# w_down of an expert in one double slot, the first gate weights by rows, and another order of the last products, squares and stores in a hybrid attention and mixture-of-experts block

## The chip, the cores and the metric

The kernel runs on one core of a Trainium2 chip. A core has five engines, each with its own instruction queue: TensorE (PE: matmuls, with the weight loads shown apart as PEld), VectorE (DVE), ScalarE (ACT), GpSimd (POOL) and SyncE (SP, which here does nothing but issue DMAs). Sixteen DMA engines move data between HBM and SBUF (the on-chip memory of 128 partitions); matmuls write into PSUM banks. The engines meet only through semaphores. The metric is the device time of one execution in microseconds.

## The reference

The input is `x` of 256 tokens by 1024 features, in fp32. Cut to what matters:

```python
h = rmsnorm(x, g1)
z = h @ w_in                      # q, k, v, gates, HGRN2 inputs, merge gates
a = nsa_mixer(z...)               # compressed, selected and windowed attention
b = hgrn2_mixer(z...)             # a gated linear recurrence
x = x + merge(a, b) @ w_out
h = rmsnorm(x, g2)
# 4 groups of 8 experts; group softmax, 2 experts of each token's group
for e in range(32):
    y = (silu(h @ w_gate[e]) * (h @ w_up[e])) @ w_down[e]   # 1024x512, 1024x512, 512x1024
    x = x + weight[:, e] * y      # zero where the token is not routed to e
out = rmsnorm(x, g_final)
```

Each expert has 2 MB of `w_gate`, 2 MB of `w_up` and 2 MB of `w_down`: 192 MB for the 32 experts, and all of it is read.

## The kernel before, in words

**Front (0 to 240 us).** The projection weights come as 1 MB stripes `raw<-in_wf` of 128x2048. Each stripe is split into two parts: ACT writes the high part (`whi`, L275), DVE the low part (`wlo`, L279), and PE multiplies with three matmuls for each pair (L416, L418, L419). `split()` keeps two stripes ahead, and `split_part` holds the ACT half of a split back until a matmul of an earlier stripe (`marks[-HOLD]`). The last stripes are `n0`, `n1` (merge gates) and `o00`, `o10`, `o01`, `o11` (`pwo`, the output projection). Norm, routing and the gather of tokens follow (`pga`, L1113).

**Experts (240 us to the end).** Eight groups `q` of four experts. A group takes `hidden(q)`: the gate product into `pg` and the up product into `pu` (both L1225 in `product`), silu and the product of both in `h`; then `prepare(q + 1)`, the routing of the next group; then `down(q)`: `py` (L1279), the weighting and the split of the result into `ys` (L1261 on ACT, L1262 on DVE), and the scatter into four PSUM banks `acc[tt][n]` (L1267; tt a tile of 128 tokens, n a half of the columns). The last group has `down_last` instead (L1293): first columns 0:512, then 512:768 and 768:1024. `finish` makes the last rmsnorm: `square` (ACT, L1334), `scaled` (DVE, L1339: acc times the row of the norm's gains), sum and power on POOL (L1345, L1346), the scaling by DVE and ACT (L1347, L1349) and four stores of 256 KB, two on SP's queue and two on ACT's.

**Weights and slots.** All expert weights go through SP's queue, which works its DMAs off in order: an issue that waits holds up all that stand behind it. `load_expert(n)` (L310, L320, L324) issues the next n pieces of a list: per group eight gate pieces, eight up pieces, eight w_down pieces, of 1 MB each (8 KB in each of 128 partitions). They lie in the pool `big` of `WSLOTS` = 25 slots of 1 MB, which the stripes and their split parts share. `product` frees four slots and asks for four pieces after each half (16 matmuls in the program, 32 in the trace, which shows two records for each), `down` likewise. How many pieces are issued during the front, and behind which stripe, is set by the table `EARLY` and by one call of `load_expert(25 - sum(EARLY.values()))`. The last group's w_down is loaded by columns: 0:512 of all four row blocks (1 MB each, runs of 2 KB), then two times 256 columns (512 KB each, runs of 1 KB).

**Order.** Each engine's instruction order is laid down at build time by a scheduler that follows the program order and estimated times. Within `overflow()` (L1404), a branch that is not taken in this run, the slot `y` is used too, so the first write of the output tile `y` (L1339) waits until SP's queue has passed that branch.

Of the kernel before, what the change touches and what calls it, by code (L numbers as in the profile page):

```python
# [163 lines left out]
WSLOTS = 25  # L164
# [7 lines left out]
CUTS = [slice(0, 256), slice(256, 512)]  # L172
GATE_V = (0, 0)
EARLY = {"m20": 1, "h1": 3, "o00": 1, "m21": 1, "m00": 2, "o11": 2, "m01": 2, "m31": 2, "h0": 1, "o01": 2}
# [5 lines left out]
def tile_block(ctx, tc, x, xp, xa, xb, wf, wcmp, vec, rows, consts, lmask, w_gate, w_up, w_down, out, dbg=None, manual=False):  # L180
# [11 lines left out]
    def slot(name, dtype=F32):  # L192
        return big.tile([128, 2048], dtype, tag="w", name=name)

# [99 lines left out]

    pieces = []
    for q in range(NE // 4):
        for i in range(6):
            pieces += [(4 * q + e, i) for e in range(4)]

    def load_expert(n=1):  # L300

        for _ in range(n):
            if pieces:
                e, i = pieces.pop(0)
                hf = i % 2
                t = slot("we")
                if i < 4:
                    store, src = ((WG, w_gate), (WU, w_up))[i // 2]
                    store[e, hf] = t.rearrange("p (k c) -> p k c", k=4)
                    nc.sync.dma_start(store[e, hf], src[e].rearrange("(p k) c -> p k c", k=8)[:, 4 * hf:4 * hf + 4])  # L310
                elif e >= NE - 4:

                    w = t.rearrange("p (k c) -> p k c", k=4)
                    WD[e, hf] = w
                    for c in CUTS if hf else [WHOLE]:
                        tails.append((w, e, hf, c))
                else:
                    w = t.rearrange("p (k c) -> p k c", k=2)
                    WD[e, hf] = w
                    nc.sync.dma_start(w, w_down[e].rearrange("(p k) c -> p k c", k=4)[:, 2 * hf:2 * hf + 2])  # L320
                if len(tails) == 12:
                    tails.sort(key=lambda x: (x[2], x[3].start, x[1]))
                    for w, e, hf, c in tails:
                        nc.sync.dma_start(w[:, :, c], w_down[e, :, 512 * hf:512 * hf + 512].rearrange(  # L324
                            "(p k) c -> p k c", k=4)[:, :, c])
                    tails.clear()

    tails = []
# [14 lines left out]
    hh_, hl_ = slot("hh_", F32R), slot("hl_", F32R)  # L343
# [8 lines left out]
    rr = cp.tile([128, 2], F32, name="rr")  # L352
    cbr = cp.tile([128, 2, 8, 5], F32, name="cbr")
# [866 lines left out]
    def product(q, W, p):  # L1220

        for hf in range(2):
            for k in range(4):
                for e in range(4):
                    i = PE.matmul(p[32 * e:32 * e + 32], xes[q][:, 4 * hf + k, 32 * e:32 * e + 32], W[4 * q + e, hf][:, k],  # L1225
                                  start=hf == 0 and k == 0, stop=hf == 1 and k == 3, skip_group_check=True)
            load_expert(4)
# [45 lines left out]
    def down(q):  # L1273
        py = [bank(t, "py") for t in ("ns", "pj")]
        for kh in range(2):
            for j in range(2):
                for n in range(2):
                    for e in range(4):
                        PE.matmul(py[n][32 * e:32 * e + 32], hTs[q][:, 2 * kh + j, 32 * e:32 * e + 32],  # L1279
                                  WD[4 * q + e, kh][:, j, 512 * n:512 * n + 512], start=kh == 0 and j == 0,  # L1280
                                  stop=kh == 1 and j == 1, skip_group_check=True)
            load_expert(4)
# [5 lines left out]
    def down_last(q):  # L1288

        def columns(n, c, p):  # L1290
            for j in range(4):
# [136 lines left out]
```

## Time and profile before

| | |
|---|---|
| median of three runs | 687.94 us (687.25 to 688.8) |
| the profiled execution | 686.17 us, of which the span from first to last instruction is 684.2 us |
| mean granted TensorE clock | 0.946 of full speed |
| busy: PE, PEld, DVE, ACT, POOL | 84%, 46%, 31%, 21%, 5% of the span |
| moved by DMA | 238.85 MB, mean 349 GB/s |

Engine shares are means over the whole span, and the stages differ: up to 240 us the projections and attention run, behind it the experts. What lies between the span and the run's own time (2 us) is start and end outside the instructions. In the rows further down, "idle before <- X" tells what ended an engine's idle time before an instruction.

### The profile page before, as it was taken

The numbers are of one execution on the slowest core, as the hardware profiler recorded it, in microseconds if no ns is written. First come the engines' busy times: TensorE is split into PE (matmuls) and PEld (weight loads), VectorE is DVE, ScalarE is ACT, GpSimd is POOL, SyncE is SP. The second block draws the span as 40 slices with busy tenths as digits, with TensorE's granted clock in tenths as the row PEclk, the third lists the DMA queues.
The fourth block names the chain that finished last, engine by engine and source line by source line (L and its number), as shares of the span: only waits on it lengthen the run. The fifth ranks groups of instructions, "written<-read, shape, count | busy, mean of one in ns | idle before, by whom it ended". The sixth has DMA issues, their size and how long they took to land. (4 is left out here: it accounts for less than half of the span.)

```text
span 684.2 us, 8830 instructions
## 1 busy us (share of the span) xinstructions
PE 576.8 (84%) x3692; PEld 317.8 (46%) x3692; DVE 212.1 (31%) x430; ACT 145.2 (21%) x231; POOL 32.5 (5%) x47
## 2 busy tenths in 40 slices
PE   8999999999999999987779668787766877796674
PEld 7988778888997834342132114223211421231111
DVE  5886656668567431121011002201100210110012
ACT  6433558474364210100000000000000000000002
POOL 0323202000000100000000000000000000000001
PEclk9999999999999999999899989989998998898898
DMA  8963534846748989999999999999999999999993
GB/s 340 406 249 123 185 124 152 341 182 230 287 165 309 421 332 420 419 420 420 420 420 420 417 421 420 420 420 420 420 418 419 420 421 420 421 419 421 406 366 114
DMA packets 39788, 238.85 MB, mean 349 GB/s; under 512 B 4032, under 2 KB 8640, under 8 KB 12608
## 3 DMA queue, kind: packets, MB, share of 16 engines
q1 hardware_dynamic: 39312, 237.19, 85.9%
q10 hardware_dynamic: 432, 1.05, 0.4%
q8 instruction: 31, 0.51, 0.3%
q14 instruction: 13, 0.11, 0.0%
HBM read 237.17 MB, written 1.05 MB: 348 GB/s over the span
## 5 line engine op out<-in xcount | busy, mean ns | idle before, releaser
L1225 PE MATMUL pu<-we,xe 128*32 128x512 f32 x512 | 98.3, 715 | 35.0 <-DMA we<-in_w_up 31.8
L1225 PE MATMUL pg<-we,xe 128*32 128x512 f32 x512 | 95.4, 689 | 35.2 <-DMA we<-in_w_gate 35.2
L1279 PE MATMUL py<-we,hT 128*32 128x512 f32 x448 | 76.2, 596 | 9.4 <-DMA we<-in_w_down 9.3
L1249 DVE SCALAR_TENSOR_TENSOR h<-pu,wv,h 128x512 f32<-128x512 f32 x8 | 8.7, 1089 | 227.3 <-PE pu L1225 227.3
L279 DVE TENSOR_TENSOR wlo<-raw,whi 128x2048 fp32r<-128x2048 f32 (+3 forms) x34 | 67.6, 1995 | 23.3 <-ACT whi L275 23.2
L1225 PEld LDWEIGHTS pu<-we,xe 128*32 128x32 f32 x512 | 21.3, 127 | 107.2 <-DMA we<-in_w_up 60.2
L1225 PEld LDWEIGHTS pg<-we,xe 128*32 128x32 f32 x512 | 20.5, 123 | 105.0 <-DMA we<-in_w_gate 65.3
L1261 ACT ACTIVATE ys<-py,wv 128x512 fp32r<-128x512 f32 (+1 forms) x17 | 11.2, 662 | 264.4 <-PE py L1279 232.4
L275 ACT ACTIVATE whi<-raw 128x2048 fp32r<-128x2048 f32 (+3 forms) x34 | 56.1, 1663 | 37.4 <-PE pxs L419 12.5
L419 PE MATMUL pws<-hh__93,wlo 128*128 128x256 f32 x192 | 48.4, 284 | 0.5 <-DVE wlo L279 0.5
L418 PE MATMUL pws<-hl__94,whi 128*128 128x256 f32 x192 | 48.5, 284 | 0.0
L1279 PEld LDWEIGHTS py<-we,hT 128*32 128x32 f32 x448 | 19.8, 109 | 59.6 <-issue 35.5
L1262 DVE SCALAR_TENSOR_TENSOR ys<-py,wv,ys 128x512 fp32r<-128x512 f32 (+1 forms) x17 | 12.2, 719 | 93.0 <-ACT ys L1261 92.3
L1243 ACT ACTIVATE h<-pg,wv 128x512 f32<-128x512 f32 x8 | 9.2, 1148 | 134.9 <-PE pg L1225 134.8
L419 PEld LDWEIGHTS pws<-hh__93,wlo 128*128 128x128 f32 x192 | 36.7, 191 | 0.7 <-DVE wlo L279 0.7
L418 PEld LDWEIGHTS pws<-hl__94,whi 128*128 128x128 f32 x192 | 36.7, 191 | 0.2 <-issue 0.2
L416 PE MATMUL pws<-hh__93,whi 128*128 128x256 f32 x192 | 33.3, 293 | 0.9 <-ACT hh__93 L375 0.9
L1113 PE MATMUL pga<-lm,x 128*128 128x128 f32 x256 | 30.3, 276 | 0.0
L418 PE MATMUL pxs<-wlo,hh__93 128*128 128x512 f32 (+1 forms) x80 | 29.8, 375 | 0.0
L419 PE MATMUL pxs<-whi,hl__94 128*128 128x512 f32 (+1 forms) x80 | 29.5, 372 | 0.0
L1113 PEld LDWEIGHTS pga<-lm,x 128*128 128x128 f32 x256 | 29.3, 192 | 0.2 <-DVE lm L1104 0.2
L416 PEld LDWEIGHTS pws<-hh__93,whi 128*128 128x128 f32 x192 | 26.6, 191 | 4.7 <-issue 1.9
(246 smaller groups left out, 655.4 us busy)
## 6 DMA issues: line engine op xcount, KB each, us to landing
we<-in_w_gate SPq DMA_DIRECT2D x64, 1024.0 KB, 19.9
we<-in_w_up SPq DMA_DIRECT2D x64, 1024.0 KB, 19.9
we<-in_w_down SPq DMA_DIRECT2D x60, 1024.0 KB, 19.9
raw<-in_wf SPq DMA_DIRECT2D x27, 1024.0 KB, 5.2
we<-in_w_down SPq DMA_DIRECT2D x8, 512.0 KB, 9.4
raw<-in_wf SPq DMA_DIRECT2D x2, 560.0 KB, 11.8
raw<-in_wf SPq DMA_DIRECT2D x2, 512.0 KB, 5.7
x<-in_x SPq DMA_DIRECT2D x2, 512.0 KB, 9.4
```

What stands on the lines that cost most here:

```text
L275: i = S.activation(his[n][:, c], raws[n][:, c], AF.Copy)
L279: splits.append((i, V.tensor_tensor(los[n][:, c], raws[n][:, c], his[n][:, c].bitcast(F32), op=OP.subtract)))
L416: PE.matmul(out_, lh, rh, start=start and i == 0, stop=False, skip_group_check=True)
L418: PE.matmul(out_, lh, rl, start=False, stop=False, skip_group_check=True)
L419: last = PE.matmul(out_, ll, rh, start=False, stop=stop and i == n - 1, skip_group_check=True)
L1113: i = PE.matmul(pgs[q, n][:, 128 * k:128 * k + 128], xv[:, tt, 512 * n + 128 * k:512 * n + 128 * k + 128], sel[q][:, tt], start=tt == 0 an ...
L1225: i = PE.matmul(p[32 * e:32 * e + 32], xes[q][:, 4 * hf + k, 32 * e:32 * e + 32], W[4 * q + e, hf][:, k], start=hf == 0 and k == 0, stop=h ...
L1243: S.activation(h, pg.rearrange("p (c j) -> p c j", j=4), AF.Silu, scale=r)
L1249: V.scalar_tensor_tensor(h, pu.rearrange("p (c j) -> p c j", j=4), r, h, op0=OP.mult, op1=OP.mult)
L1261: return (S.activation(hi[:, c], p[:, c], AF.Copy, scale=wv), V.scalar_tensor_tensor(lo[:, c], p[:, c], wv, hi[:, c].bitcast(F32), op0=OP. ...
L1262: V.scalar_tensor_tensor(lo[:, c], p[:, c], wv, hi[:, c].bitcast(F32), op0=OP.mult, op1=OP.subtract))
L1279: PE.matmul(py[n][32 * e:32 * e + 32], hTs[q][:, 2 * kh + j, 32 * e:32 * e + 32], WD[4 * q + e, kh][:, j, 512 * n:512 * n + 512], start=kh ...
```

## The change

- **Slots.** The pool has 17 slots of 1 MB and four "pairs" of 2 MB, the same sum. A split stripe's two parts lie in one pair, and so do the two parts of the normed input (`hhl`). The whole w_down of an expert lies in one pair and comes by one DMA of 2 MB (16 KB in each partition). `down(q)` runs its products over all four row blocks, gives the four pairs back at its end and then asks for four pieces.
- **First group.** Its gate weights come as eight pieces by row block `k`: each has that row block of all four experts (2 KB runs). The gate product of group 0 frees one slot and asks for one piece after each four matmuls. The order of the first group is eight gate pieces, three up, one w_down, four up, three w_down, one up, and `EARLY` is set anew.
- **Last w_down.** Per expert row blocks 0 and 1 with all columns (1 MB, 8 KB runs), then row blocks 2 and 3 in columns 0:512 (512 KB, 2 KB runs), 512:768 and 768:1024 (256 KB each, 1 KB runs).
- **End.** `down_last` multiplies row blocks 0 and 1 of all three column spans first, then 2 and 3 span by span. Squares and `scaled` of columns 0:768 are made in parts as the spans come; `finish` squares the last 256 columns (tile 0 on ACT, tile 1 on DVE), and scales in parts on DVE and ACT. One store of 512 KB per token tile, both on SP's queue.

```diff
-WSLOTS = 25
+WSLOTS = 17
+PAIRS = 4
+LAST = [(slice(0, 2), slice(0, 1024)), (slice(2, 4), slice(0, 512)), (slice(2, 4), slice(512, 768)), (slice(2, 4), slice(768, 1024))]
...
+    def pair(name, dtype=F32):
+
+        return big.tile([128, 4096], dtype, tag="w2", bufs=PAIRS, name=name)
...
-            his[n] = slot("whi", F32R)[:, :WIDTH[n]]
-            los[n] = slot("wlo", F32R)[:, :WIDTH[n]]
+            his[n], los[n] = [t[:, :WIDTH[n]] for t in two(pair("wsp", F32R), 2048)]
...
+                if kind == "k":
+                    WG[i] = slot("we").rearrange("p (e c) -> p e c", e=4)
+                    nc.sync.dma_start(WG[i], w_gate[0:4].rearrange("e (p k) c -> p e k c", k=8)[:, :, i])
...
+                    WD[e] = pair("wd").rearrange("p (k c) -> p k c", k=4)
+                    if e < NE - 4:
+                        nc.sync.dma_start(WD[e], w_down[e].rearrange("(p k) c -> p k c", k=4))
+                    elif e == NE - 1:
+                        load_last()
...
+                if 4 * hf + k in W and q == 0:
+                    load_expert(1)
+            if 4 * hf not in W or q:
+                load_expert(4)
...
+        for i in range(3):
+            products(i, (0, 1))
+        for i, (n, c) in enumerate(spans):
+            products(i, (2, 3))
+            if i < 2:
+                ys = parts_of()
+            weighted(q, n, c, py[i], ys)
+            scatter(q, n, c, ys)
+            if i < 2:
+                for tt in range(2):
+                    square(tt, n, c)
+                    scaled(tt, n, c)
...
+        c = CUTS[1]
+        ss, f = [st[:, 8 + tt:9 + tt] for tt in range(2)], [st[:, 10 + tt:11 + tt] for tt in range(2)]
+        S.activation(scr[0][:, c], acc[0][1][:, c], AF.Square, scale=1 / 32, accum_out=ss[0])
+        V.tensor_copy(scr[1][:, c], acc[1][1][:, c])
+        V.scalar_tensor_tensor(scr[1][:, :256], acc[1][1][:, c], 1 / 1024, scr[1][:, c], op0=OP.mult, op1=OP.mult,
+                               accum_out=ss[1])
...
+            nc.sync.dma_start(out[128 * tt:128 * tt + 128, :], y)
...
-    load_expert(25 - sum(EARLY.values()))
+    load_expert(20 - sum(EARLY.values()))
```

SP's queue at the end of the front stands so before (`raw` a stripe, `x_2058` the input tile, `we` a slot with expert weights):

```order
L261 DMA raw<-in_wf 128x2048 x4
L223 DMA x_2058<-in_xp 128x1024 x2
L310 DMA we<-in_w_up 128x2048 x4
L320 DMA we<-in_w_down 128x2048 x8
L310 DMA we<-in_w_gate 128x2048 x8
L310 DMA we<-in_w_up 128x2048 x8
```

and so in the changed kernel (`wd` a pair with the w_down of one expert):

```order
L267 DMA raw<-in_wf 128x2048 x3
L324 DMA wd<-in_w_down 128x4096
L267 DMA raw<-in_wf 128x2048
L229 DMA x_2030<-in_xp 128x1024 x2
L320 DMA we<-in_w_up 128x2048 x4
L324 DMA wd<-in_w_down 128x4096 x3
L320 DMA we<-in_w_up 128x2048
L320 DMA we<-in_w_gate 128x2048 x8
```

The first w_down piece now stands ahead of the last stripe, and the last piece of group 0 ahead of the first gate piece of group 1 is an up piece of 1 MB. On VectorE, early in the front (about 14 to 24 us of the trace before; `prx` is a PSUM tile with the first norm's row factors, `rxb` its copy, `hg` a projection of HGRN2), this is the order before:

```order
L384 SCALAR_TENSOR_TENSOR xa,st<-x 128x1024
L497 TENSOR_TENSOR lbt<-vc__70 128x4
L391 TENSOR_SCALAR rxt<-cs,st 128x128 x2
L500 TENSOR_SCALAR lbt<-lbt 128x4
L279 TENSOR_TENSOR wlo<-raw,whi 128x2048
L400 COPY rxb<-prx 128x256
L516 TENSOR_TENSOR hg_301<-pws,rxb 128x512
```

and this in the changed kernel:

```order
L503 TENSOR_TENSOR lbt<-vc__70 128x4
L390 SCALAR_TENSOR_TENSOR xa,st<-x 128x1024
L506 TENSOR_SCALAR lbt<-lbt 128x4
L397 TENSOR_SCALAR rxt<-cs,st 128x128 x2
L406 COPY rxb<-prx 128x256
L285 TENSOR_TENSOR wsp<-raw,wsp 128x2048 x2
L522 TENSOR_TENSOR hg_299<-pws,rxb 128x512 x2
```

The copy of `prx` now stands ahead of the low part of that stripe (`wsp<-raw,wsp`) instead of behind it. On TensorE, the last instructions before are:

```order
L1293 MATMUL py<-we,hT 32x512 x16
L1293 MATMUL py<-we,hT 32x256 x5
L1267 MATMUL acc<-ys,sT 128x512 x2
L1293 MATMUL py<-we,hT 32x256 x4
L1267 MATMUL acc<-ys,sT 128x512 x2
L1293 MATMUL py<-we,hT 32x256 x16
L1267 MATMUL acc<-ys,sT 128x256 x2
L1293 MATMUL py<-we,hT 32x256 x4
L1267 MATMUL acc<-ys,sT 128x256 x2
L1293 MATMUL py<-we,hT 32x256 x3
L1267 MATMUL acc<-ys,sT 128x256 x4
```

and in the changed kernel:

```order
L1306 MATMUL py<-wd,hT 32x512 x8
L1306 MATMUL py<-wd,hT 32x256 x16
L1306 MATMUL py<-wd,hT 32x512 x8
L1306 MATMUL py<-wd,hT 32x256 x5
L1277 MATMUL acc<-ys,sT 128x512 x2
L1306 MATMUL py<-wd,hT 32x256 x4
L1277 MATMUL acc<-ys,sT 128x512 x2
L1277 MATMUL acc<-ys,sT 128x256 x4
L1306 MATMUL py<-wd,hT 32x256 x7
L1277 MATMUL acc<-ys,sT 128x256 x4
```

Half of each span's products stand ahead of the others; of the last span seven products and its four scatter matmuls stand behind the scatter of the span before it.

## Rows read from the trace of the kernel before

**Rows 1.** The page's second part: the span in 40 equal slices of 17.1 us, busy tenths of PE and of the DMA engines, and GB/s.

```profile
PE   8999999999999999987779668787766877796674
DMA  8963534846748989999999999999999999999993
GB/s 340 406 249 123 185 124 152 341 182 230 287 165 309 421 332 420 419 420 420 420 420 420 417 421 420 420 420 420 420 418 419 420 421 420 421 419 421 406 366 114
```

**Rows 2.** The page's sixth part: DMA issues, count, size of each, median us from issue to landing.

```profile
we<-in_w_gate SPq DMA_DIRECT2D x64, 1024.0 KB, 19.9
we<-in_w_down SPq DMA_DIRECT2D x60, 1024.0 KB, 19.9
```

**Rows 3.** Waits of SP's queue: us in total, times, longest.

```profile
SPq L310 <- DMA we<-in_w_gate: 113.9, 54, 3.3
SPq L310 <- PE pg L1225: 14.0, 7, 11.9
```

**Rows 4.** Timeline of SP's queue, 205 to 260 us: start, length of the merged group, issues.

```profile
217.50 14.95 SPq L320 DMA_DIRECT2D we<-in_w_down  x8
244.25 5.24 SPq L310 DMA_DIRECT2D we<-in_w_gate  x8
```

**Rows 5.** Stretches from the front's end into the experts: window, its length, busy us of PE, PEld, DVE, ACT and POOL, granted clock, DMA share, GB/s.

```profile
232.00:240.00 8.00, 7.54 (x84) 6.89 (x84) 5.58 (x28) 1.26 (x4) 0.81 (x2) 1.00 1.01 421
240.00:242.00 2.00, 2.00 (x23) 0.98 (x25) 1.93 (x11) 0.51 (x4) 0.00 (x0) 1.00 0.99 406
242.00:244.00 2.00, 2.00 (x24) 0.56 (x20) 1.55 (x13) 0.35 (x3) 0.00 (x0) 1.00 0.17 70
244.00:246.00 2.00, 2.00 (x24) 0.65 (x20) 0.00 (x0) 0.00 (x0) 0.00 (x0) 1.00 0.43 78
246.00:248.00 2.00, 2.00 (x20) 0.66 (x13) 0.00 (x0) 0.00 (x0) 0.00 (x0) 1.00 0.93 377
248.00:252.00 4.00, 4.00 (x39) 1.39 (x42) 0.99 (x6) 2.47 (x2) 0.00 (x0) 1.00 1.01 424
```

**Rows 6.** Timeline of PE, group 0: start, length of the merged group, instruction.

```profile
240.60 7.07 PE L1225 MATMUL pg<-we,xe 128*32 128x512 f32 x64
```

**Rows 7.** Timeline of DVE and PE early in the front, and the one wait of PE on a low part at L419 there.

```profile
18.84 2.28 DVE L279 TENSOR_TENSOR wlo<-raw,whi 128x2048 fp32r<-128x2048 f32 x1
21.05 0.41 DVE L400 COPY rxb<-prx 128x256 f32<-128x256 f32 x1
20.19 0.59 PE L399 MATMUL prx<-rxt,one 128*128 128x256 f32 x2
21.21 0.36 PE L419 MATMUL pws<-hh__93,wlo 128*128 128x256 f32 x1
PE pws L419 <- DVE wlo L279: 0.5, 1, 0.5
```

**Rows 8.** Timeline of ACT and DVE at the merge (194 to 206 us): the sigmoid of the merge gates (`mg`), the split parts and `mT`, the input of the output projection.

```profile
197.57 1.92 ACT L891 ACTIVATE mg<-mg 128x2048 f32<-128x2048 f32 x1 [1.66 <-DVE mg L886]
201.53 0.63 ACT L966 ACTIVATE mT<-mg 128x512 fp32r<-128x512 f32 x1 [0.52 <-DVE mg L964]
202.07 1.90 ACT L275 ACTIVATE whi<-raw 128x2048 fp32r<-128x2048 f32 x1
204.71 2.28 DVE L279 TENSOR_TENSOR wlo<-raw,whi 128x2048 fp32r<-128x2048 f32 x1
```

**Rows 9.** Two long stretches of the experts, in the columns of rows 5.

```profile
288.00:476.00 188.00, 144.75 (x787) 48.74 (x787) 21.71 (x48) 7.53 (x9) 0.00 (x0) 0.92 1.01 419
486.00:646.00 160.00, 119.05 (x618) 35.78 (x620) 12.93 (x28) 7.51 (x9) 0.00 (x0) 0.89 1.01 419
```

**Rows 10.** Timeline of the last group, all engines: start, length, instruction, idle time before it and what ended it.

```profile
648.89 3.62 PE L1225 MATMUL pu<-we,xe 128*32 128x512 f32 x26 [1.47 <-DMA we<-in_w_up]
659.73 3.64 PE L1293 MATMUL py<-we,hT 128*32 128x512 f32 x30 [1.01 <-DMA we<-in_w_down]
671.68 1.06 PE L1293 MATMUL py<-we,hT 128*32 128x256 f32 x12 [0.75 <-SPq L1404]
671.79 1.29 DVE L1339 TENSOR_TENSOR y<-acc,fin 128x512 f32<-128x512 f32 x2 [6.87 <-SPq L1404]
673.00 0.47 DVE L1262 SCALAR_TENSOR_TENSOR ys<-py,wv,ys 128x256 fp32r<-128x256 f32 x1
674.10 0.63 PE L1293 MATMUL py<-we,hT 128*32 128x256 f32 x6
674.79 0.47 ACT L1261 ACTIVATE ys<-py,wv 128x256 fp32r<-128x256 f32 x1 [4.84 <-PE py L1293]
675.32 1.02 PE L1267 MATMUL acc<-ys,sT 128*128 128x256 f32 x4 [0.58 <-ACT ys L1261]
676.32 0.60 ACT L1334 ACTIVATE fin<-acc 128x512 f32<-128x512 f32 x1 [1.06 <-PE acc L1267]
677.43 0.57 POOL L1346 TENSOR_TENSOR st<-st,mhalf 128x1 f32<-128x1 f32 x1
678.03 1.54 DVE L1347 SCALAR_TENSOR_TENSOR y<-acc,st,fin 128x512 f32<-128x512 f32 x2 [2.25 <-POOL st L1346]
678.81 1.13 SPq L1348 DMA_DIRECT2D out_dram<-y  x2
```

More of the change, by code (lines that the diff above doesn't have):

```diff
@@ L296, in tile_block @@
     for q in range(NE // 4):
-        for i in range(6):
-            pieces += [(4 * q + e, i) for e in range(4)]
+        g, u, d = [[(n, 4 * q + e, i) for i in range(2 if n != "d" else 1) for e in range(4)] for n in "gud"]
+        if q:
+            pieces += g + u + d
+        else:
+            pieces += [("k", 0, k) for k in range(8)] + u[:3] + d[:1] + u[3:7] + d[1:] + u[7:]
     def load_expert(n=1):
@@ L303, in load_expert, with load_last @@
             if pieces:
[L304 to L316, printed above, removed]
-                else:
[L318 to L328, printed above, removed]
+                kind, e, i = pieces.pop(0)
+                if kind == "k":
+                    WG[i] = slot("we").rearrange("p (e c) -> p e c", e=4)
+                    nc.sync.dma_start(WG[i], w_gate[0:4].rearrange("e (p k) c -> p e k c", k=8)[:, :, i])
+                elif kind != "d":
+                    store, src = {"g": (WG, w_gate), "u": (WU, w_up)}[kind]
+                    store[e, i] = slot("we").rearrange("p (k c) -> p k c", k=4)
+                    nc.sync.dma_start(store[e, i], src[e].rearrange("(p k) c -> p k c", k=8)[:, 4 * i:4 * i + 4])
+                else:
+                    WD[e] = pair("wd").rearrange("p (k c) -> p k c", k=4)
[3 more added lines that the diff above has]
+                        load_last()
+    def load_last():
+        for k, c in LAST:
+            for e in range(NE - 4, NE):
+                nc.sync.dma_start(WD[e][:, k, c], w_down[e].rearrange("(p k) c -> p k c", k=4)[:, k, c])
     load_front()
@@ L340, in tile_block @@
     nc.sync.dma_start(lmf, lmask)
-    hh_, hl_ = slot("hh_", F32R), slot("hl_", F32R)
+    hh_, hl_ = two(pair("hhl", F32R), 2048)
     hhi = hh_.rearrange("p (k t) -> p k t", k=8)
@@ L352, in tile_block @@
     rr = cp.tile([128, 2], F32, name="rr")
+    eps_ = cp.tile([128, 1], F32, name="eps_")
+    G.memset(eps_, EPS)
     cbr = cp.tile([128, 2, 8, 5], F32, name="cbr")
@@ L1274, in down @@
         py = [bank(t, "py") for t in ("ns", "pj")]
[L1275 to L1282, printed above, removed]
+        for j in range(4):
+            for n in range(2):
+                for e in range(4):
+                    PE.matmul(py[n][32 * e:32 * e + 32], hTs[q][:, j, 32 * e:32 * e + 32],
+                              WD[4 * q + e][:, j, 512 * n:512 * n + 512], start=j == 0, stop=j == 3,
+                              skip_group_check=True)
+        load_expert(4)
         for n in range(2):
@@ new lines, in scaled @@
+    def scaled(tt, n, c):
+        o = 512 * n
+        V.tensor_tensor(yo[tt][:, o + c.start:o + c.stop], acc[tt][n][:, c], fins[n][:, c], op=OP.mult)
+    def finish():
+        c = CUTS[1]
[4 more added lines that the diff above has]
+                               accum_out=ss[1])
+        last = ()
+        for tt, m in ((1, 512), (0, 256)):
+            y = yo[tt]
+            with ExitStack() as o:
+                for i in last:
+                    o.enter_context(after(i))
+                G.tensor_tensor(ss[tt], ss[tt], st[:, 4 + tt:5 + tt], op=OP.add)
+                G.tensor_tensor(f[tt], ss[tt], mhalf[:, :1], op=OP.pow)
+                i = V.scalar_tensor_tensor(y[:, 768:], acc[tt][1][:, c], f[tt], fins[1][:, c], op0=OP.mult, op1=OP.mult)
+            a = S.activation(y[:, :m], y[:, :m], AF.Copy, scale=f[tt])
+            with after(i):
+                last = a, V.tensor_scalar(y[:, m:768], y[:, m:768], f[tt], None, op0=OP.mult)
+            nc.sync.dma_start(out[128 * tt:128 * tt + 128, :], y)
```

53 lines of the change are left out of this document (14 added, 39 removed).

## The prediction

> **What bounds the kernel now.** I read the slices of the span first. From slice 15 on the DMA engines are at 9 tenths or more and the rate stands at 420 GB/s, while PE falls to 6 to 8 tenths [rows 1]. So there are two stages. Up to about 240 us PE is the bound (8 and 9 tenths in nearly every slice) and DMA has room. Behind it the weights are the bound: two stretches of 188 and 160 us moved 419 GB/s each with PE busy for 144.75 and 119.05 us of them [rows 9]. SP's waits agree: the issue of weights waits mostly for earlier weights to land [rows 3], and a piece of 1 MB lands 19.9 us after its issue [rows 2], which is eight pieces of 2.5 us. In such a stage faster compute is worth nothing; time comes only from gaps in the stream, from a slower or faster stream, and from what stands behind the last byte.
>
> The stream has a gap. The longest wait on SP's queue that is not for DMA is one of 11.9 us for the gate product [rows 3]: the last w_down pieces of group 0 are issued from 217.50 to 232.45, the next gate piece at 244.25 [rows 4]. All 25 slots are full then, and the first come free when half of the gate product of group 0, which starts at 240.60 and takes 7.07 us, is done [rows 6]. From 240 to 248 us the four windows of 2 us moved 406, 70, 78 and 377 GB/s instead of 421 [rows 5]. That is 1,506 KB short, or 3.6 us of stream.
>
> Then the tail. The last up piece releases PE at 648.89, the last w_down piece of the first column half at 659.73, the very last at 671.68 [rows 10]. So 4 MB in runs of 2 KB took 10.84 us (2.71 each MB) and 4 MB in runs of 1 KB 11.95 (2.99), against 2.50 at 419 GB/s with runs of 8 KB. From 671.68 to the end of the span at 684.2 it is compute and stores.
>
> **The change, part by part.** The sum is made against the profiled execution, 686.17 us.
>
> *Gate of group 0 by rows.* A slot now comes free after an eighth of the product: 240.60 + 0.88 = 241.5 in place of 244.1. Before, issue at 244.25 brought the flow back at about 246.2 (the window from 246 is 0.2 us short of full), 1.95 us later. So the flow would be back at 243.5 instead of 246.2: 2.7 us of the 3.6 return. The rest of group 0's stream must not be late itself; its queue order is as before but for one w_down ahead of the last stripe, so I charge it nothing. The row pieces have 2 KB runs, 0.21 us more for each MB, 1.7 us for eight; they are loaded in the front, where DMA has room. If that cover were gone, 1.7 us would be the price.
>
> *What moves in the front.* PE's own instructions stay. But two places of the order shift work ahead of what PE needs. First, VectorE's copy of `prx` now stands before a low part. `prx` is done at 20.19 + 0.59 = 20.78 and the copy takes 0.41; the low part, 2.28 long, then ends at 23.5 instead of 21.1, and PE asks for it at 21.2 [rows 7]. PE loses 2.3 us there, less the 0.5 us that it waits for a low part in the front anyway: 1.8. Second, at the merge ScalarE has the sigmoid and then mT at 201.53, with the split of the next stripe behind it [rows 8]; in the new order splits stand between the sigmoid and mT. One is 1.90 us and part of it fills idle time and a table load; I take 1.0, bounds 0 and 1.9, and as much again is possible on VectorE (2.28). Together gate 0 starts 2.5 us later (bounds 0 and 4, since PE idles little and any order with some slack would absorb part). In a PE-bound front each of these microseconds moves the gate product, and with it the return of the flow. What is left of the gap's gain: 2.7 - 2.5 = 0.2 us, bounds +2.7 and -1.3.
>
> *The double slots.* For the steady state I ask whether the stream can starve. `down(q)` frees all four pairs at its end. The next w_down is loaded 16 pieces, 40 us of stream, later, and even 20 us of issue ahead leave 20 us; PE is behind the last landing by some 7 us (32 matmuls as in the gate product). So no wait. Group q's down products can start only when the fourth pair is there; PE has 20% idle time [rows 9] and catches up under the next gate pieces. Cost nothing; if PE had no idle time, the 7 us would show at every group.
>
> *Runs of 16 KB.* No row shows them. From 1 KB to 2 KB runs a MB gets 0.28 us cheaper for 512 runs less, from 2 KB to 8 KB 0.21 us for 384 less: 0.00055 us for a run both times. On that line 16 KB saves 64 runs a MB, 0.035 us. For the 48 MB of w_down that stream in groups 1 to 6 that is 1.7 us. The bound on the other side is 0: that the hardware cuts at 8 KB already. Two equal slopes point to the line, so I take 1.7 and keep 0.
>
> *Last w_down.* 4 x 2.50 + 2 x 2.71 + 2 x 2.99 = 21.4 us against 22.8: 1.4 us less, if 256 KB pieces behave as 512 KB ones (bounds 0.8 and 1.4, see the rivals).
>
> *Behind the last byte (call it T, 671.6).* Before, 26 recorded matmuls and scatters end at 674.73, T + 3.1. In the new order seven products of the last span remain, of which some five wait for the last piece: ten records at 1.06/12 us, T + 0.9. That is 2.2 us earlier. But VectorE's `y` still waits for SP to pass the branch (671.79, 6.87 us idle) [rows 10], and then takes 1.29 us, which lies beside the products and ScalarE's `ys`. Behind `ys` (0.47 twice) come two more gain products of 256 columns (0.65 together, half of 1.29) before PE may write the bank again; the squares are halves (0.2 less); the scaling in parts is queued on two engines (0.3 more); a store is 512 KB instead of 256 (262 KB at 400 GB/s, 0.65 us more). So 2.2 - 1.4 = 0.8, and I take 0.7; bounds 0 and 1.5.
>
> **Sum:** 0.2 + 1.7 + 1.4 + 0.7 = 4.0 us less, 682.2 for an execution like the profiled one. The median shown is 1.8 us above that execution, so 683.9 as a median.
>
> **A rule that speaks against it.** The tail's last eight pieces become 256 KB. The row nearest to them is the second half of the old tail, 2.99 us for each MB in pieces of 512 KB, against 2.71 in pieces of 1 MB [rows 10]; runs and sizes change together there, so the 0.28 may be the price of pieces, 0.14 each, instead of runs. Then eight of 256 KB cost 0.82 each, 6.5 instead of 6.0 us. The Trainium skill ("DMA: Bandwidth & Descriptors", section "Measured (HBM→SBUF, 128 partitions, SWDGE, issued from GpSimd)") says to batch DMAs to at least 1 MiB for 75% of peak, and its section on the anatomy of one DMA gives some 2.0 us fixed per DMA. By that page an estimate for eight pieces, taken one by one, is 16 us more at the tail, and the change would be slower; the trace disagrees as far as it goes, with 512 KB pieces at 351 GB/s.
>
> **Rivals.**
> - *16 KB runs bring nothing.* For it: no row above 8 KB. Sum 2.3 us, 685.6.
> - *The front eats it.* If the new order costs 5 us instead of 2.5 (both splits at the merge in full, 1.9 + 2.28, besides the copy), the gap's term is -2.3: 686.4, or 688.1 without the gain of the runs. For it: PE idles for hardly anything in the front. Against it: the split runs two stripes ahead.
> - *Slower by the pairs.* The split parts had any of 25 slots; now one pair is held by `hhl`, so three are left and a fourth split must wait for PE to end a stripe. If that made PE wait at the stripes, gate 0 would start later still. It decides the sign when gate 0 is 7.9 us late instead of 2.5 (4.0 + 1.4 more): some 0.2 us at each of 27 stripes. At 10 us late: 691.4. Against it: two stripes ahead need only three pairs.
> - *Slower by small pieces.* Each piece costs a fixed time that those in flight do not hide. With no overlap at all it is the 1.95 us between issue and flow of the gap [rows 4, 5], 15.6 us for eight: 699.5. It decides the sign at 0.68 us each (4.0 + 1.4 over eight). Against it: 351 GB/s with pieces of 512 KB. The page named above speaks for it.
>
> **How the numbers follow.** About 0.2%, 1.4 us, can be told from no change. Forecast 0.45; no gain by runs 0.30; front eats it 0.15; pairs 0.07; pieces 0.03. Faster holds the forecast, nearly all of the second and a third of the third: 0.77. Same: most of the third's rest, 0.12. Slower: 0.11. The range goes from all bounds good but one (2.7 in the gap: 681.4, with the tail's 1.5: 680.6) up to between the third's two times, 687.4, and leaves out some 2 in 10. The forecast's own range is 682 to 686.
>
> **What would show it.** The first gate issue of group 1 about 1 us behind the start of gate 0, and the gap's windows with less than 3 us lost; gate 0 at 243; a wait of PE for VectorE of 2 us near 21 us; steady GB/s at 425 if the runs matter, 420 if not; 21.4 us from the last up piece to the last w_down piece; 11.8 us from there to the end. Wrong it is if gate 0 starts past 245, if PE waits for w_down so long that weights' issues wait for PE in the middle groups, or if the last eight pieces take over 0.85 us each.

## The result and the profile after

The changed kernel takes 682.69 us (median; 682.09 to 683.06) against 687.6 us for the kernel before beside it: a ratio of 0.9933, with a 95% interval of 0.992 to 0.9947. Timed twice more it gave 682.59 (0.9931, 0.9918 to 0.9943) and 682.18 (0.9915, 0.9895 to 0.9935). Forecast were 683.9 us, 4.0 less; measured are 4.6 to 5.1 us less.

The slices after, to be held against [rows 1]: busy tenths of PE and DMA, GB/s.

```profile
PE   8899999999999999978567866977776785678564
DMA  8991642744658999999999999999999999999992
GB/s 341 394 385 65 237 166 93 261 138 148 258 187 291 431 416 421 427 425 419 420 430 421 420 428 421 421 420 430 420 421 425 425 420 420 430 419 422 417 383 107
```

The two stages are the same, but the middle slices now reach 425 to 430 GB/s again and again. The stretches that answer to [rows 5] and [rows 9], in the same columns:

```profile
242.00:244.00 2.00, 2.00 (x23) 1.58 (x25) 1.13 (x3) 0.00 (x0) 0.00 (x0) 1.00 0.97 414
244.00:246.00 2.00, 2.00 (x24) 0.62 (x20) 2.00 (x20) 0.85 (x6) 0.00 (x0) 1.00 0.96 401
246.00:248.00 2.00, 2.00 (x24) 0.65 (x20) 0.47 (x3) 0.00 (x0) 0.00 (x0) 1.00 1.01 401
288.00:476.00 188.00, 139.24 (x815) 48.80 (x808) 21.71 (x48) 7.53 (x9) 0.00 (x0) 0.91 1.01 424
486.00:646.00 160.00, 114.97 (x647) 36.61 (x646) 12.94 (x28) 7.51 (x9) 0.00 (x0) 0.92 1.01 422
```

The gap is gone: 414, 401 and 401 GB/s stand where 70, 78 and 377 stood, some 0.2 us short of a full stream instead of 3.6. And the steady stream went from 419 GB/s in both stretches to 424 and 422. But gate 0 is later. Its product on PE and the first gate issue of group 1 on SP's queue, for [rows 4, 6]:

```profile
243.52 7.07 PE L1232 MATMUL pg<-we,xe 128*32 128x512 f32 x64
244.65 6.34 SPq L320 DMA_DIRECT2D we<-in_w_gate  x8
```

The issue follows gate 0 by 1.13 us instead of 3.65, yet it comes at 244.65, 0.4 us later than before, since gate 0 came 2.9 us later. The w_down pieces of 2 MB, and the last and smallest pieces of the last w_down (the page's sixth part: count, size, us from issue to landing):

```profile
wd<-in_w_down SPq DMA_DIRECT2D x28, 2048.0 KB, 24.7
wd<-in_w_down SPq DMA_DIRECT2D x8, 256.0 KB, 7.9
```

From the landings in the trace each execution can be cut into four stretches, which leave nothing out: the start to the last gate piece of group 1; from there to the last up piece of group 7; from there to the last w_down piece; from there to the span's end. With a second profile of the kernel before (b0_again) and a second and third of the changed one (a0_again, a2_again), in us (the spans with one more digit than the page gives):

| | gate 0 starts | last gate piece of group 1 | to the last up piece | to the last w_down piece | to the end | span |
|---|---|---|---|---|---|---|
| before | 240.60 | 267.98 | 380.86 | 22.79 | 12.53 | 684.16 |
| before, again | 241.32 | 268.37 | 381.11 | 22.76 | 12.51 | 684.74 |
| changed | 243.52 | 268.81 | 379.16 | 21.14 | 12.04 | 681.16 |
| changed, again | 242.74 | 268.25 | 378.87 | 21.27 | 12.01 | 680.40 |
| changed, third | 242.81 | 268.30 | 379.08 | 21.05 | 12.49 | 680.92 |
| difference of the means | +2.1 | +0.3 | -1.9 | -1.6 | -0.3 | -3.6 |

So the whole gain of the profiled executions lies in the stream and the tail, and the front with the gap gave nothing. Two of the columns need care. In every trace two landings come 0.7 us or more later than their size gives, and all behind them stay late by as much (the last section). The kernel before has one such landing in the second column (258.0) and one in the third (481.5), the changed kernel has both of its own in the third (423.6 and 640.5). If each is taken out by what it stands above the usual distance, which is an estimate from these landings, the second column's difference is +1.4 and the third's -3.7. The late landings cost 2.4 us in all before and 3.0 after, so the sum changes by 0.6 alone.

The spans differ by 3.6 us, the medians by 4.6 to 5.1: both profiled executions of the kernel before (686.17 and 686.75) are faster than its medians, while those of the changed kernel (683.06, 682.30 and 682.82) lie near theirs. What the other executions of the kernel before have that these two have not, no trace shows, so 1 to 1.5 us of the gain by medians is not accounted for.

### The profile page after: what moved, and what is told of

Same layout as the page of the kernel before. It is cut to its first block, busy times and chain, and to the rows that moved or that the text cites. A ratio compares the mean times of both kernels' runs of the same rounds, so it can differ in the third digit from the quotient of the medians.

```text
span 681.2 us, 8766 instructions
## 1 busy us (share of the span) xinstructions
PE 561.8 (82%) x3692; PEld 319.8 (47%) x3692; DVE 213.5 (31%) x437; ACT 144.7 (21%) x233; POOL 32.7 (5%) x50
## 4 chain that ended last, share of the span: by engine, by line
DMA 61%; PE 18%; DVE 1%; issue 0%; ACT 0%; POOL 0%; POOLq 0%; DVEq 0%; SPq 0%
DMA we<-in_w_gate 23%; DMA we<-in_w_up 20%; DMA wd<-in_w_down 18%; PE pws L422 3%; PE pws L424 3%; PE pws L425 3%; PE pwo L422 1%; PE pwo L425 1%; PE pwo L424 1%; PE pno L876 1%; PE pnt L853 1%; PE psc L814 1%; PE pga L1119 1%; PE pg L1232 1%; PE prt L1040 1%; PE acc L1277 0%
## 5 line engine op out<-in xcount | busy, mean ns | idle before, releaser
L1232 PE MATMUL pu<-we,xe 128*32 128x512 f32 x512 | 89.5, 631 | 42.2 <-DMA we<-in_w_up 38.8
L1288 PE MATMUL py<-wd,hT 128*32 128x512 f32 x448 | 85.9, 683 | 29.5 <-DMA wd<-in_w_down 29.5
L1232 PE MATMUL pg<-we,xe 128*32 128x512 f32 x512 | 80.6, 660 | 18.3 <-DMA we<-in_w_gate 18.3
L285 DVE TENSOR_TENSOR wsp<-raw,wsp 128x2048 fp32r<-128x2048 f32 (+3 forms) x34 | 68.3, 2014 | 32.0 <-ACT wsp L281 31.7
L281 ACT ACTIVATE wsp<-raw 128x2048 fp32r<-128x2048 f32 (+3 forms) x34 | 56.3, 1664 | 42.9 <-PE pws L425 16.9
L1288 PEld LDWEIGHTS py<-wd,hT 128*32 128x32 f32 x448 | 20.8, 118 | 88.4 <-DMA wd<-in_w_down 43.7
L425 PE MATMUL pws<-hhl,wsp 128*128 128x256 f32 x192 | 49.7, 289 | 2.1 <-DVE wsp L285 2.1
L424 PE MATMUL pws<-hhl,wsp 128*128 128x256 f32 x192 | 50.0, 291 | 0.0
L425 PEld LDWEIGHTS pws<-hhl,wsp 128*128 128x128 f32 x192 | 38.0, 198 | 2.3 <-DVE wsp L285 2.3
L424 PEld LDWEIGHTS pws<-hhl,wsp 128*128 128x128 f32 x192 | 38.2, 199 | 0.2 <-issue 0.2
L422 PE MATMUL pws<-hhl,wsp 128*128 128x256 f32 x192 | 34.8, 302 | 1.4 <-ACT hhl L381 1.4
L422 PEld LDWEIGHTS pws<-hhl,wsp 128*128 128x128 f32 x192 | 27.8, 199 | 4.9 <-ACT hhl L381 2.3
L424 PE MATMUL pxs<-wsp,hhl 128*128 128x512 f32 (+1 forms) x80 | 29.7, 375 | 0.0
L425 PE MATMUL pxs<-wsp,hhl 128*128 128x512 f32 (+1 forms) x80 | 29.6, 374 | 0.0
## 6 DMA issues: line engine op xcount, KB each, us to landing
wd<-in_w_down SPq DMA_DIRECT2D x4, 512.0 KB, 17.1
```

Source lines behind the costliest of these rows:

```text
L281: i = S.activation(his[n][:, c], raws[n][:, c], AF.Copy)
L285: splits.append((i, V.tensor_tensor(los[n][:, c], raws[n][:, c], his[n][:, c].bitcast(F32), op=OP.subtract)))
L422: PE.matmul(out_, lh, rh, start=start and i == 0, stop=False, skip_group_check=True)
L424: PE.matmul(out_, lh, rl, start=False, stop=False, skip_group_check=True)
L425: last = PE.matmul(out_, ll, rh, start=False, stop=stop and i == n - 1, skip_group_check=True)
L1288: PE.matmul(py[n][32 * e:32 * e + 32], hTs[q][:, j, 32 * e:32 * e + 32], WD[4 * q + e][:, j, 512 * n:512 * n + 512], start=j == 0, stop=j ...
```

## The experiments

The theory: four terms, each by its own mechanism, as in the forecast: rows bring the flow back early, the later gate 0 takes that back, runs of 16 KB quicken the stream, the tail's stream and compute give the rest. The rivals are named with each run.

**Gate weights by rows, alone, on the kernel before (b1_gate_rows).**

```diff
+                if e == "k":
+                    WG[i] = t.rearrange("p (e c) -> p e c", e=4)
+                    nc.sync.dma_start(WG[i], w_gate[0:4].rearrange("e (p k) c -> p e k c", k=8)[:, :, i])
...
+                if 4 * hf + k in W and q == 0:
+                    load_expert(1)
...
```

> The kernel before with one part of the change alone: the first group's eight gate pieces by row block, freed after each four matmuls of the gate product. Slots, order of the queue and tail as before, and VectorE's order too. Theory (the gap of 3.6 us is due to the late release, and without the later gate 0 it can be had back): first gate issue of group 1 about 1 us behind gate 0 at 241.5 to 242, flow back at 243.5 instead of 246.2, 2 to 2.7 us less: 685 to 685.6. Rival (the gap returns elsewhere, since group 1's pieces then run into full slots a little later): 687 or more.

Measured: 685.13 us against 687.14, a ratio of 0.9973 (0.9962 to 0.9984). SP's queue and the stretches there:

```profile
242.09 6.34 SPq L315 DMA_DIRECT2D we<-in_w_gate  x8
242.00:244.00 2.00, 2.00 (x26) 0.53 (x17) 1.91 (x18) 0.71 (x6) 0.00 (x0) 1.00 0.75 229
244.00:246.00 2.00, 2.00 (x24) 0.64 (x20) 0.00 (x0) 0.00 (x0) 0.00 (x0) 1.00 0.97 397
```

With gate 0 at 240.96 the issue comes 1.13 us behind it. The last gate piece of group 1 lands at 265.56, 2.6 us before the mean of the two profiles of before, the last up piece of group 7 at 647.54, 1.6 us before it, and the time fell by 2.0. Late landings (the last section) stand at other places here, which is part of why the lead differs; taken together the rows alone are worth some 2 us, and the rival falls.

**Gate weights by halves again, in the changed kernel (e2_gate_halves).**

```diff
-            pieces += [("k", 0, k) for k in range(8)] + u[:3] + d[:1] + u[3:7] + d[1:] + u[7:]
+            pieces += g + u[:3] + d[:1] + u[3:7] + d[1:] + u[7:]
```

> The changed kernel with the first group's gate weights by halves per expert again, so that the gate product of group 0 frees four slots after each half instead of one after each four matmuls. Everything else stays, the order on PE, VectorE and ScalarE too. Theory (rows bring the flow back earlier): the first gate issue of group 1 comes at 243.5 + 3.5 = 247 instead of 244.65, the flow returns at 249, and as group 0's last piece lands at 248.9 some 2 us of stream are lost: 684.7. Rival (group 0's own stream ends so late now that the pieces behind it are not waited for): within 0.5 us of 682.7.

Measured: 683.62 us, 1.0 above the changed kernel's 682.6; the profiled execution is the slowest of its five. SP's queue and the gap:

```profile
247.10 5.46 SPq L320 DMA_DIRECT2D we<-in_w_gate  x8
246.00:248.00 2.00, 2.00 (x24) 0.65 (x20) 0.39 (x2) 0.00 (x0) 0.00 (x0) 1.00 0.33 131
248.00:250.00 2.00, 2.00 (x24) 0.52 (x16) 0.00 (x0) 0.00 (x0) 0.00 (x0) 1.00 0.91 254
```

The gap is back, 131 and 254 GB/s in two windows, and the last gate piece of group 1 lands at 270.66 instead of 268.3 to 268.8. Rows are needed, the rival falls; their worth is between the 1.0 of the times (the theory had 2.0) and the 1.9 to 2.4 of the landings.

**w_down in runs of 8 KB (e1_runs8k).**

```diff
-                        nc.sync.dma_start(WD[e], w_down[e].rearrange("(p k) c -> p k c", k=4))
+                        for r in range(2):
+                            nc.sync.dma_start(WD[e][:, 2 * r:2 * r + 2], w_down[e].rearrange(
+                                "(p k) c -> p k c", k=4)[:, 2 * r:2 * r + 2])
```

> The changed kernel with one thing undone: each expert's w_down comes by two DMAs of 1 MB in runs of 8 KB into the same pair, instead of one of 2 MB in runs of 16 KB. The pairs, the order of the products and the tail stay. Theory (a run costs 0.00055 us whatever its length, so 16 KB runs save 0.035 us a MB): the 48 MB of groups 1 to 6 stream 1.7 us slower, time 682.7 + 1.7 = 684.4, and the steady stretch from 288 to 476 us falls from 424 back to 419 or 420 GB/s. Rival (the higher rate comes from something else, such as fewer waits on SP's queue or a different mix of transfers): time stays within 0.5 us of 682.7 and the rate at 422 to 424.

Measured: 683.0 us, 0.4 above the changed kernel. By time alone the rival would have won. The trace says otherwise: both long stretches move 421 GB/s, and from the last gate piece of group 1 to the last up piece it takes 380.98, 1.9 us more than the changed kernel. The front of the profiled execution was early, gate 0 at 241.17, but one execution doesn't explain a median of five (682.63 to 683.15). That left the time open, so the same edit was made once more, beside its own standard (below).

**The copy behind the low part (e4_copy_order).** The order of VectorE that the forecast blamed for a wait of PE is put back with one constraint.

```diff
-        V.tensor_copy(rxb, prx[:, :256])
+        with after(splits[-1][1]):
+            V.tensor_copy(rxb, prx[:, :256])
```

> The changed kernel with one constraint added: the copy of prx on VectorE stands behind the low part of that stripe again, as in the kernel before. PE's order stays. Theory (the 2.1 us wait of PE near 21 us and the lower granted clock behind it, 0.66 from 25 to 30 us, are why gate 0 starts 2.9 us late): gate 0 starts at 240.6 to 241.5, SP's issues in the front move along, the whole stream ends 2 to 2.9 us earlier, 679.8 to 680.7. Rival (the loss is absorbed later, or gate 0 is late by the order at the merge and the chunk products): gate 0 stays at 243 or later and the time within 0.6 us of 682.7.

Measured: 681.32 us, 1.4 less than the changed kernel, and gate 0 at 241.73: between the theory and the rival in both. PE's wait for the low part is gone, but PE now waits near 27 us for the read of the HGRN2 projection (`hg`), which stands behind the next low part and holds a PSUM bank:

```profile
PE pws L423 <- DVE hg L523: 1.3, 1, 1.3
```

**The read before the next low part, too (e5_order).**

```diff
+            if first_hg:
+                s.enter_context(after(first_hg.pop()))
             splits.append((i, V.tensor_tensor(los[n][:, c], ...
...
+            first_hg[:] = [V.tensor_tensor(H.f[:, sl]...
```

> The changed kernel with the constraint of the last experiment and one more: the next stripe's low part stands behind the first read of the HGRN2 projection, as in the kernel before (this read then frees the PSUM bank for which PE waited 1.3 us in the profile of the version with the first constraint alone). Theory: that wait goes, gate 0 some 0.8 us earlier than 241.7 at equal clock, 680.5. Rival (the front then waits elsewhere): 681.3 within 0.4.

Measured: 682.58 us (680.94 to 684.12). No gain, 0.9 us above the rival's upper bound, and gate 0 at 243.87. In this execution the next stripe landed at 25.56 (24.07 in e4_copy_order's, 23.31 in that of before), and PE waits 1.5 us for its low part. The order is that of the kernel before; what is late is the load.

**The copy behind the low part, beside the changed kernel (a2_again, e4_again).** Neither has a new edit.

> The changed kernel once more, as the standard for the three runs beside it on the same chip. Both theories: 682.6 within 0.5 us.

> The version with the copy of prx behind the low part, once more beside the changed kernel. Theory (2.1 us of PE's wait are taken away, part comes back as a wait for a PSUM bank): 1.0 to 1.8 us faster than the changed kernel beside it, gate 0 about 1.8 us earlier where the early clock is the same. Rival (the 681.3 came from executions with a better early clock): within 0.5 us of the changed kernel.

Measured: 682.18 and 681.84 us, a difference of 0.3 that their ranges (681.13 to 682.82 and 680.96 to 683.86) cover, as the rival has it. The wait for `hg` is longer here:

```profile
PE pws L423 <- DVE hg L523: 3.1, 1, 3.1
```

The stripe landed at 25.59 in this execution, 1.5 us later than in the first, and gate 0 came at 244.19. So the wait of 2.1 us is there in every profile with the new order, but without it PE runs into the next wait, which was longer where the stripe landed later. By the place of this copy alone gate 0 did not come back reliably. What it is worth in time stays open: the eleven executions of this version in both runs have a mean of 681.8 us, the fifteen of the changed kernel 682.3, and single executions of either lie up to 2 us from their mean.

**Both, with runs of 8 KB (e6_copy_8k).** The edits of e4_copy_order and e1_runs8k together.

> The version with the copy behind the low part, and w_down by two DMAs of 1 MB in runs of 8 KB instead of one of 2 MB in runs of 16 KB. Theory (the runs are worth 1.7 to 2.0 us of stream; in the first such run an early front hid it): from the last gate piece of group 1 to the last up piece of group 7 some 381.0 us instead of 379.0, and the time 1.5 to 2 us above the version beside it. Rival (the runs change the profile but not the time): within 0.6 us of it.

Measured: 683.96 us, 2.1 above e4_again beside it. The two stretches, first of this version, then of e4_again:

```profile
288.00:476.00 188.00, 140.26 (x809) 48.30 (x802) 21.82 (x49) 7.52 (x9) 0.00 (x0) 0.90 1.01 421
486.00:646.00 160.00, 117.10 (x644) 36.04 (x644) 12.94 (x28) 7.51 (x9) 0.00 (x0) 0.91 1.01 421
```

```profile
288.00:476.00 188.00, 139.20 (x805) 48.09 (x798) 21.02 (x47) 8.15 (x10) 0.00 (x0) 0.91 1.01 423
486.00:646.00 160.00, 115.51 (x644) 36.92 (x644) 12.94 (x28) 7.51 (x9) 0.00 (x0) 0.90 1.01 422
```

From the last gate piece of group 1 to the last up piece: 381.02 against 379.08, 1.9 us. In the changed kernel a w_down of 2 MB lands 4.90 us behind the one before it, with 8 KB runs 2 x 2.49. The longer runs are worth 1.9 us in both pairs of traces, with late landings at the same places in each pair. In the time one pair gave 2.1 and the other 0.4, so there the size is open.

Two readings are left to check against these traces. The edit makes two DMAs of one besides halving the runs. But at the tail pieces of half the size with the same runs are not dearer: 2.71 us for each MB in pieces of 512 KB with runs of 2 KB, as in pieces of 1 MB before, and 2.86 in pieces of 256 KB with runs of 1 KB against 2.99 in pieces of 512 KB. So it is the runs and not the number of DMAs, as far as the tail's sizes tell. And the runs are not all that quickened the stream: with 8 KB runs both long stretches still move 421 GB/s, where the kernel before moves 419 [rows 9]. So the 1.9 in the table's third column equals the runs' worth by accident. By the estimate given with the table, some 1.9 us more come from another part of the change, which no run here takes alone, and the one late landing more in that column costs about as much.

**The old tail whole (e3_old_tail)**, and **the old end alone (e7_old_finish)**, of both the first lines of the edit. The first puts back the load by columns, the products, the squares and the stores; the second only what comes after the products.

```diff
-LAST = [(slice(0, 2), slice(0, 1024)), (slice(2, 4), slice(0, 512)), ...
+LAST = [(slice(0, 4), slice(0, 512)), (slice(0, 4), slice(512, 768)), (slice(0, 4), slice(768, 1024))]
...
```

> The changed kernel with the tail undone: the last w_down by columns, the last products, squares, scaling and the four stores as in the kernel before. Theory (both halves of the tail gained: 1.6 us of DMA and 0.45 us behind the last byte): 682.7 + 2.1 = 684.8. Rival (only the stream counts, the new compute and stores gain nothing that lasts): 684.3 or less, with 12.1 us or less from the last landing to the end of the span.

```diff
-            if i < 2:
+            if i < 1:
                 for tt in range(2):
-                    square(tt, n, c)
-                    scaled(tt, n, c)
+                    square(tt, n)
+                    scaled(tt, n)
+        square(0, 1)
+        square(1, 1)
         finish()
...
```

> The changed kernel with the old end alone: squares of the second column half whole, scaling and four stores of 256 KB on two queues as before; the new load order of the last w_down and the new order of the products stay. Theory (the earlier products are worth 2.2 us, and the end in parts with one store per tile costs part of it, 1.4 by the forecast's sum): 0.5 to 1.4 us faster than the changed kernel, some 11 us from the last landing to the end of the span instead of 12.0. Rival (the end in parts is what gains the 0.5 us): 0.3 us or more slower, 12.5 us.

Measured: 684.06 us for the first, 1.4 above the changed kernel; last w_down piece 22.33 us behind the last up piece instead of 21.1 to 21.3, and 12.27 us to the end. By its time this is the rival's side (684.3 or less), by the end just past the rival's 12.1; the tail as a whole is worth 1.4 us in the time. The second takes 681.41, 0.8 below the changed kernel beside it (682.18), and 0.9907 of the kernel before (0.9886 to 0.9927): the lowest ratio of all versions, though the interval covers the ratios of the version with the copy moved (0.9914 and 0.9912). It needs 11.24 us from its last landing (668.24) to the end. Its end:

```profile
670.64 1.02 PE L1277 MATMUL acc<-ys,sT 128*128 128x256 f32 x4 [0.59 <-ACT ys L1271]
672.75 0.57 POOL L1357 TENSOR_TENSOR st<-st,mhalf 128x1 f32<-128x1 f32 x1
673.35 1.54 DVE L1358 SCALAR_TENSOR_TENSOR y<-acc,st,fin 128x512 f32<-128x512 f32 x2 [2.25 <-POOL st L1357]
674.13 1.14 SPq L1359 DMA_DIRECT2D out_dram<-y  x2
```

and the changed kernel's, whose last piece lands at 669.12:

```profile
669.70 1.06 PE L1306 MATMUL py<-wd,hT 128*32 128x256 f32 x14
671.73 0.95 DVE L1347 TENSOR_TENSOR y<-acc,fin 128x256 f32<-128x256 f32 x2
672.20 1.04 PE L1277 MATMUL acc<-ys,sT 128*128 128x256 f32 x4 [1.44 <-DVE y L1347]
673.62 0.55 POOL L1364 TENSOR_TENSOR st<-st,mhalf 128x1 f32<-128x1 f32 x1
675.10 0.48 DVE L1365 SCALAR_TENSOR_TENSOR y<-acc,st,fin 128x256 f32<-128x256 f32 x1 [0.93 <-POOL st L1364]
675.93 1.09 SPq L1369 DMA_DIRECT2D out_dram<-y  x2
```

Measured from the last landing, the last scatter starts at 2.40 us with the old end and at 3.08 with the new one, where it waits 1.44 us for the gain products (`y`, L1347) that read the bank; the first store is issued at 5.89 and 6.81. So the new order of products is worth some 1.3 us (12.5 to 11.24), and the end in parts takes 0.8 of it back in two profiles of the changed kernel and 1.25 in the third.

**The two kernels once more, for a second profile.**

> The changed kernel unchanged, once more, as the standard for the runs beside it. Both theories: 682.7 within 0.5 us; a second profile shows whether gate 0 at 243.5 and the lower clocks from 9 to 13 and from 25 to 30 us come again (theory: they differ between executions of one program, gate 0 between 241 and 244) or stay (rival: 243.5 within 0.3).

> The kernel before once more, unchanged, for a second profile. Theory (the granted clock right behind PE's first wait for hh, and behind later waits, falls in some executions of the same program and not in others, which shifts gate 0 by 1 to 3 us): gate 0 starts at another time than 240.60 if the windows from 9 to 13 us show a clock under 1.00, and at 240.6 if not. Rival (only the changed order lowers the clock there): clock 1.00 in all early windows and gate 0 at 240.6 within 0.3 us.

Measured: 682.59 us for the changed kernel and 686.75 (one execution) for the one before, with gate 0 at 242.74 and at 241.32. The early clock does differ between executions of one program; the last section has the rows.

## Why the prediction was right, step by step

The median lies 1.2 us under the forecast of 683.9, and the sum of 4.0 us is near the 3.6 between the spans. Part of that is luck: terms that were too large and a gain that the forecast did not have nearly cancel. The 1.8 us between the profiled execution and the median did not carry over either, since the changed kernel's profiled executions lie near its medians.

- **The gap by rows: 2.7 us back.** The mechanism is right, the issue comes 1.13 us behind gate 0 as foreseen. The size was some 0.7 too large: 2.0 us in the time of the kernel with that part alone, 1.6 to 2.6 by its landings.
- **Gate 0 2.5 us later.** Measured 2.1 (means). The size held, the parts did not. The wait at the copy was foreseen as 2.3 and is 2.1, the longest of PE's waits in the changed kernel's front:

```profile
PE pws L425 <- DVE wsp L285: 2.1, 1, 2.1
PE pws L422 <- ACT hhl L381: 1.4, 1, 1.4
PE pw L374 <- POOL ones L409: 1.2, 1, 1.2
PE pht L634 <- DVE sg L622: 0.9, 1, 0.9
PE pho L611 <- DVE sg L622: 0.7, 1, 0.7
```

  In the kernel before, three of these stood so, and none for `pho`:

```profile
PE pw L368 <- POOL ones L403: 1.1, 1, 1.1
PE pws L416 <- ACT hh__93 L375: 0.9, 1, 0.9
PE pht L628 <- DVE sg L616: 0.2, 1, 0.2
```

  The 1.0 us at the merge was wrong in sign: counted on PE's matmuls, the changed kernel is 3.46 us late at the end of the merge gates and 2.91 late in the output projection, so it gained 0.5 there. In its place stand waits in the attention and HGRN2 part that the forecast did not look at (`pht` and `pho` for `sg`, 1.6 us together); by PE's matmuls the changed kernel falls back by 0.9 us there, from 2.78 to 3.69. The 2.91 hold a difference of the clock, too: against b0_again, with a low clock in the same early stretch (the last section), it is 2.20. And the experiments add that the copy is not a lone cause: with it put back PE waits at the next place.
- **What is left of the gap: 0.2 us gained.** Measured 0.3 lost, or 1.4 with the late landing of the kernel before taken out. The term's flaw is the 0 charged for group 0's own stream: its last piece landed at 248.93 instead of 245.30 in the profiled executions. Issues in the front hang on PE too: SP's queue waits 11.1 us for `pwo` there, in two waits (11.2 before), and `pwo` is late. That this alone makes the 3.6 us was not tried.
- **16 KB runs: 1.7 us.** Measured 1.9 by landings in two pairs of traces, 0.4 and 2.1 by time. By the landings the rival with 0 falls. The line held from 2 to 8 and 16 KB; at its 1 KB end the changed kernel's own pieces give 0.15 us less for each MB from 1 to 2 KB, not 0.28, so that the two equal slopes were in part chance. The other gain of the stream, some 1.9 us with runs of 8 KB, is in no term of the forecast.
- **Last w_down: 1.4 us.** Measured 1.6. Four pieces of 512 KB took 1.35 us each and eight of 256 KB 0.71, by landings at 658.00, 663.41 and 669.12: less than the 0.75 forecast. The rule of the Trainium skill ("DMA: Bandwidth & Descriptors", section "Measured (HBM→SBUF, 128 partitions, SWDGE, issued from GpSimd)") is to batch DMAs to at least 1 MiB for 75% of peak. The trace does not bear it out here: on SP's queue, with eight in flight, pieces of 256 KB ran at 367 GB/s, 87% of the 421 with 1 MB, and the trace decides.
- **Behind the last byte: 0.7 us.** Measured 0.3 (0.5 in two profiles of three). Both halves were mis-sized: the products gave 1.3 instead of 2.2, since the last span starts behind the scatter of the span before, at 669.70, 0.6 us after the landing; the end in parts costs 0.8 to 1.25 instead of 1.4.
- **The double slots: nothing.** No loss is seen: SP's queue waits for PE's gate product in the middle groups as it did before (14.0 us in all in both kernels, 11.9 of it at the gap before and 9.4 there after), but the rate there rose; and PE had idle time to catch up (139.24 us busy of 188).
- **The rivals.** Pairs that starve the splits: the waits of PE are single ones of 2.1 us and less, no row of 0.2 us at each stripe; gate 0 is far from 7.9 us late. The front that eats the gain: gate 0 is 2.1 us late, not 5 (its parts in the forecast add up to 6.0). Small pieces: see above.

## What to carry to other kernels

A slot that is freed in smaller steps brings a starved stream back at once, but the scheduler's new order around it may take the gain: compare the order of the engines that were not touched, and cost each instruction that moved. Longer contiguous runs paid here even above 8 KB, 0.04 us for each MB, near what the rows for 2 and 8 KB give. A difference between two landings can hold a late landing or miss one: look where those lie before a column is put down to one cause. At the tail, cut the loads small but keep the last chain short: here the gain products that share a bank with the last scatter lengthened it.

## What the runs showed of the hardware

- **The granted clock in the front.** In the stretch from 9 to 13 us (columns as in [rows 5]), of b0_again, of the changed kernel and of a0_again:

```profile
9.00:13.00 4.00, 4.00 (x24) 4.00 (x24) 3.77 (x9) 3.92 (x8) 0.00 (x0) 0.64 1.02 411
```

```profile
9.00:13.00 4.00, 4.00 (x24) 4.00 (x24) 3.96 (x9) 4.00 (x9) 0.00 (x0) 0.62 1.01 404
25.00:30.00 5.00, 5.00 (x31) 5.00 (x30) 2.12 (x1) 3.05 (x2) 0.78 (x2) 0.66 1.03 431
```

```profile
9.00:13.00 4.00, 3.97 (x29) 3.51 (x30) 3.96 (x10) 4.00 (x9) 0.00 (x0) 1.00 1.01 406
```

  A mean of 0.62 or 0.64 is 1.2 GHz for most of the stretch and 2.4 GHz for the rest: 24 matmuls instead of the 34 of before's first profile, where it was 1.00. The same program had 1.00 and 0.64 (before), and 0.62 and 1.00 (changed). In all fourteen profiles the low mean came where PE had waited 1.2 to 1.6 us for the normed input just before, and 1.00 where it had waited 0.5 to 1.0. Behind the wait of 2.1 us the stretch from 25 to 30 us had 0.66 to 0.76 in five profiles and 1.00 in two. Two executions of one program that differ in the stretch from 9 to 13 us have gate 0 0.7 us (before) and 0.8 us (changed, again) apart. e1_runs8k, with 1.00 in both stretches and the same matmuls in the front, has it 2.35 us ahead of the changed kernel's first profile, with a low clock in both. But a higher clock need not arrive at gate 0: a2_again also had 1.00 in both, waited 1.0 us for `hg` instead, and came at 242.81. So the clock can outweigh some of the terms above; no run sets it.
- **Landings that come late now and then.** In every trace two landings stand some 0.7 to 1.7 us further apart than their size gives, about 217 to 224 us from one to the next (258.0 and 481.5 before, 423.6 and 640.5 after; e2_gate_halves has a third at 253.0, where the flow comes back after its gap). From 636 to 641 us in the changed kernel the windows of 1 us around such a place still moved 393 to 426 GB/s, so the DMA engines had not all stopped. One of them lies ahead of the end of group 1's gate pieces in the kernel before and in no profile of the changed kernel. So a comparison by one landing is good to about 1 us, and the +0.3 and -1.9 of the table's second and third columns carry that; versions whose late landings stand at the same places, as those with runs of 8 and 16 KB, can be compared closer. The page's third part lists a queue with 31 packets of 16 KB each, of the kind "instruction" (the same line in all runs):

```profile
q8 instruction: 31, 0.51, 0.3%
```

  Each of these packets took 0.9 to 1.9 us. In all fourteen traces the two late landings come 2 to 7 us behind the start of such a packet, and the two packets are eight apart: the 15th and 23rd in both profiles of the kernel before, the 21st and 29th in all others. That the fetches are the cause is not shown; no run changed them.
